# State-space layer's input projections: from 256-column products in threes to a 512-column product and a 256-column one

## The chip, the cores and the metric

One core of one Trainium2 chip runs the whole model in one launch. The metric is the device time of one execution in microseconds (us). Engines are named as in the profile: PE is TensorE's matmul, PEld its weight load, DVE VectorE, ACT ScalarE, POOL GpSimd, SP the queue that issues the DMAs.

## What is computed

The reference runs a first block (attention of two kinds, then a mixture of sixteen experts) on 256 tokens of width 1024, and then two layers of a second block, each a mixer and a feed-forward part. The mixer of the first of these layers is a state-space layer, and it is the part that matters here, cut to its core:

```python
proj = u @ w_in                       # [256,1024] @ [1024,5152]
z   = proj[..., :2048]                # gate
xbc = proj[..., 2048:2048+3072]       # x (2048), B (512), C (512)
xbc = silu(causal_dwconv(xbc, conv_w, conv_b))      # four taps along the tokens
y = ssd_chunked_scan(xs, dt, a, bm, cm) + d_skip * xs
g = y * silu(z), normalised in 4 groups of 512 channels
return g @ w_out
```

All matrix products of this layer are taken in float32 accuracy by splitting each operand into a high part and a low part that TensorE multiplies at full rate: w·h is about wh·hh + wh·hl + wl·hh.

## The kernel before

A weight matrix arrives in **pages** of 1 MiB: `wpage` loads 1024 rows by 256 columns as a tile of 128 partitions by 8 blocks by 256. `split` makes the page's high part `wh` by a cast on ACT (L231) and its low part `wl` by a subtraction on DVE (L232). There are three buffers for each part, so the cast of a page waits until TensorE has done with the third page before it. The activations `hx` lie in one tile of 8 blocks, each with 256 columns of the high part and, right behind them, 256 columns of the low part; `hx[k][0]`, `hx[k][1]` and `hx[k][2]` are the high part, the low part and both together.

`c_proj` takes one page. For each of its two chunks of 128 output channels and each of 8 blocks it issues three products of 256 columns (`three`, L243 to L245): wh with the high part, wh with the low part, wl with the high part. These are 48 matmuls, all into one PSUM bank (two chunks by 256 tokens). In the state-space layer (function `ssd`) nineteen pages go this way: eleven by `xpage` (three of B and C; a fourth is computed elsewhere, as `led[1]`; and eight of x) and eight by `z_group`. `xpage` then runs the convolution straight from the PSUM bank (`conv2`: two ACT operations, L1363, and six DVE operations, L1368), and a Silu on ACT writes the result to its place. `z_group` runs the Silu straight from PSUM into `zs`, of which there is one buffer for all four groups.

`c_proj2` is there already and is used for the up projection of both feed-forward parts. It takes 32 matmuls for a page: wh with both activation parts at once (512 columns, L1335) and wl with the high part (256 columns, L1338). Each chunk has a bank of its own. A copy on ACT (L1342) brings the second half of the bank to SBUF and an addition on DVE (L1343) adds the first half to it.

PSUM has eight banks: two with the tag `cm`, two `cs`, and four accumulators (`ca00` to `ca11`) for the layer's output projection, `down`. In `ssd` the accumulators are allocated by the caller before the layer begins, and the first product goes into them in `out_group(0)`, far into the layer.

The order of the layer in the program: three pages of B and C, x of group 0, decay factors, z of group 0; then for each group g `scan(g)`, the pages of x of group g+1, `scan_end(g)` (gate, sum of squares, norm; its last reading of `zs` is L1616), the pages of z of group g+1. `out_group(0)` follows the z pages of group 2, `out_group(1)` comes within group 3, the other two at the end. A scheduler lays out each engine's queue from this order ahead of the run, and mixes what is independent: the products of the scan stand in TensorE's queue among those of the next pages. Each queue is then worked off strictly in its order. `tc.issue_after(i)` puts what is traced under it behind instruction i of the same engine.

Of the kernel before, what the change touches and what calls it, by code (L numbers as in the profile page):

```python
# [9 lines left out]
F32 = mybir.dt.float32  # L10
# [4 lines left out]
AF = mybir.ActivationFunctionType  # L15
# [152 lines left out]
def tile_model(ctx, tc, A, out):  # L168
# [40 lines left out]
    def wpage(w, c0, n, k0=0, k=8):  # L209

        return page([128, k, n], w[k0 * 128:(k0 + k) * 128, c0:c0 + n].rearrange("(k p) n -> p k n", p=128))
# [23 lines left out]
    last_mm = [None]  # L235
# [801 lines left out]
    def cm(name="cm"):  # L1037
        return psC.tile([128, 512], F32, name=name, tag="cm", bufs=2)
# [283 lines left out]
    def c_proj(pg, ps, hx, parts=1):  # L1322
        wh, wl = split(pg, parts=parts)
        for c in range(pg.shape[2] // 128):
            three(ps[:, 256 * c:256 * c + 256],
                  [(wh[:, k, 128 * c:128 * c + 128], wl[:, k, 128 * c:128 * c + 128]) for k in range(8)], hx, True, True)

    def c_proj2(pg, names, hx, out_):

        wh, wl = split(pg)  # L1330
        for c in range(pg.shape[2] // 128):
            ps = (cm, cs)[c % 2](names)
            cc = slice(128 * c, 128 * c + 128)
            for k in range(8):
                wide = lambda: pe.matmul(ps, lhsT=wh[:, k, cc], rhs=hx[k][2], start=(k == 0), stop=(k == 7))  # L1335
                if k == 0:
                    wide()
                last_mm[0] = pe.matmul(ps[:, :256], lhsT=wl[:, k, cc], rhs=hx[k][0], start=False, stop=False)  # L1338
                if k:
                    last_mm[0] = wide()  # L1340
            o = out_[:, 256 * c:256 * c + 256]
            act.copy(o, ps[:, 256:])  # L1342
            dve.tensor_tensor(o, ps[:, :256], o, ALU.add)  # L1343

    def down(acc_, items, first, last, pl=None):

        ws = [(split(pg, pl, bufs=2) if pl and i else split(pg), pairs, pg.shape[1]) for i, (pg, pairs) in enumerate(items)]
        its = list(enumerate(ws))

        for t, n, (i, ((wh, wl), pairs, n_)) in [(0, n, x) for x in its for n in range(2)] + \  # L1350
                [(1, n, x) for n in range(2) for x in its]:
            ns = slice(512 * n, 512 * n + 512)
            three(acc_[t][n], [sl(pairs[a], lambda u: u[:, nat(t)]) for a in range(n_)],
                  [(wh[:, a, ns], wl[:, a, ns]) for a in range(n_)],
                  first and i == 0, last and i == len(ws) - 1)

    def rpage(w, r0, a=2):
        return page([128, a, D], w[r0:r0 + 128 * a].rearrange("(a p) n -> p a n", p=128))
# [73 lines left out]
            dn(13, 14, 15, pl=fp)  # L1432
            return next_layer(acc_, A["norm_ffn_post_2"][i], *((A["norm_mix_pre_2"][1], lru_lead) if i == 0 else ()))

    def ssd(hx, acc_, led):
        with ExitStack() as es:
            sp3 = es.enter_context(tc.tile_pool(name="ssd_y", bufs=1, reuse_waits="tile"))
            es2 = es.enter_context(ExitStack())
            sp2 = es2.enter_context(tc.tile_pool(name="ssd", bufs=1, reuse_waits="tile"))
# [28 lines left out]
            def xpage(c0, dst):  # L1468

                if c0 == 2048:  # L1470
                    ps = led[1]
                else:
                    ps = (cs if c0 >= 2048 and c0 % 512 else cm)("xbc")
                    c_proj(wpage(w, 2048 + c0, 256), ps, hx)
                y = sp2.tile([128, 2, S], F32, name="cvs", tag="cvs", bufs=2)
                conv2(y, ps, lambda c, a: C("ssd_conv_w_2", 24 * a + c0 // 128 + c),
                      lambda c: C("ssd_conv_b_2", c0 // 128 + c), 4)
                act.activation(out=dst, in_=y, func=AF.Silu)

            xs, zs, ys = {}, {}, {}  # L1480

            def x_group(g):
                xs[g] = sp2.tile([128, 4, S], F32, name="xs", tag="xs", bufs=2)
# [3 lines left out]
            def z_group(g):  # L1487
                zs[g] = sp2.tile([128, 4, S], F32, name="zs", tag="zs", bufs=1)
                for i in range(2):
                    ps = cm("z")  # L1490
                    c_proj(wpage(w, 512 * g + 256 * i, 256), ps, hx)
                    act.activation(out=zs[g][:, 2 * i:2 * i + 2], in_=ps.rearrange("p (c n) -> p c n", c=2), func=AF.Silu)

            for i in range(4):
                xpage(2048 + 256 * i, bc[:, 2 * i:2 * i + 2])
# [122 lines left out]
                ys[g] = split(sq, sp3, "ys", 2, dve if g == 3 else pool, parts=2 if g == 3 else 1)  # L1618

            def out_group(g, pl=None):  # L1620
                down(acc_, [(rpage(A["ssd_w_out_2"][0], 512 * g + 256 * b),
                             [sl(ys[g], lambda u: u[:, 2 * b + a]) for a in range(2)]) for b in range(2)], g == 0, g == 3,
                     pl)
# [3 lines left out]
            for g in range(4):  # L1627
                scan(g)
                if g < 3:
                    x_group(g + 1)  # L1630
                else:
                    out_group(1)
                scan_end(g)
                if g < 3:
                    z_group(g + 1)
                if g == 1:
                    out_group(0)
            out_group(2)
            root_table(sp3, ys[3][0].bitcast(F32)[:, 0, 0:1])
            out_group(3)  # L1640
# [115 lines left out]
            es2.close()  # L1756
            return next_layer(acc_, A["norm_mix_post_2"][1], A["norm_ffn_pre_2"][1], up_lead(1))

    acc0 = accs()
    for t, (xg, v) in enumerate(first):  # L1760
        dve.tensor_scalar(x1[:, t], xg, inv_root(rows2, v[1], D, v[0]), None, ALU.mult)
    xps_.close()
    rw2.close()
    hx, led = ssd(hx, acc0, [ps[0] for _, ps in lead])
    hx, led = ffn(0, hx, led)
    hx, led = lru(hx, led)
    ffn(1, hx, led)
# [18 lines left out]
```

## Time and profile before

| | |
|---|---|
| median of 3 runs | 2274.14 us (2273.88 to 2277.45) |
| the profiled execution's own time | 2269.94 us |
| its span | 2268.1 us |
| busy over the span: PE, PEld, DVE, ACT, POOL | 84%, 61%, 45%, 35%, 11% |
| state-space layer, from its first projection product to its last output product | 1402.1 to 1607.6 us |

The busy shares are averages over stages with different limits: for some 900 us in the middle the expert weights stream in and DVE and ACT are nearly idle. So the rows further down are of the state-space layer's stretch, and of one stretch of the feed-forward part where the other form of the projection runs. Times inside the trace are microseconds from the span's start.

### The profile page before, as it was taken

Reading aid. Unit: us, or ns where it says so; the run is one execution under the profiler, and the core shown is the slowest. Engines: PE = TensorE matmul, PEld = TensorE weight load, DVE = VectorE, ACT = ScalarE, POOL = GpSimd, SP = SyncE. Lnnn points to the kernel's source line nnn. Section 1 sums busy time; section 2 is a strip of 40 time slices with the busy share of each in tenths; the row PEclk is TensorE's granted clock in tenths of the full one; section 3 lists DMA queues with packets and bytes.
Section 4 is the critical chain, followed back from the end, with each engine's and each line's share of the span. In section 5 each row is a group of like instructions: output and inputs, shape, how many; then the busy total and the mean of one; then the engine's idle time right before and its main releaser. Section 6 shows DMA issues by size and latency. Waiting matters only on the chain.

```text
span 2268.1 us, 31933 instructions
## 1 busy us (share of the span) xinstructions
PE 1915.4 (84%) x13582; PEld 1372.4 (61%) x13582; DVE 1017.0 (45%) x1537; ACT 799.7 (35%) x1203; POOL 244.4 (11%) x174
## 2 busy tenths in 40 slices
PE   7999999987666666665666758999999999999998
PEld 4989998842222222121222216987888889888887
DVE  7867664420000000000000005868767767877775
ACT  2445454420000000000000004655666667666564
POOL 0100013100000000000000003010222222032222
PEclk9999999999878888788879788999999999999999
DMA  9357675789999999999999998434565556456552
GB/s 325 113 186 252 215 240 190 273 354 427 426 426 427 425 426 426 426 427 426 426 426 425 426 427 295 151 129 132 175 195 184 188 167 216 142 194 196 185 186 84
DMA packets 202539, 644.30 MB, mean 284 GB/s; under 512 B 8086, under 2 KB 145430, under 8 KB 169754
## 3 DMA queue, kind: packets, MB, share of 16 engines
q1 hardware_dynamic: 202396, 642.25, 74.5%
q8 instruction: 107, 1.75, 0.3%
q14 instruction: 36, 0.29, 0.0%
HBM read 640.91 MB, written 1.05 MB: 283 GB/s over the span
## 4 chain that ended last, share of the span: by engine, by line
PE 54%; DMA 39%; DVE 4%; ACT 2%; issue 1%; POOL 0%; SPq 0%; DVEq 0%; ACTq 0%; POOLq 0%
DMA epage<-in_w_gu 24%; DMA epage<-in_w_dn 14%; PE up L1335 10%; PE up L1338 5%; PE ca L245 4%; PE ca L244 4%; PE ca L243 3%; PE qk L245 2%; PE qk L244 2%; PE qk L243 2%; PE lead L1254 2%; PE xbc L243 1%; PE v L244 1%; PE v L245 1%; PE v L243 1%; PE xbc L244 1%
## 5 line engine op out<-in xcount | busy, mean ns | idle before, releaser
L232 DVE TENSOR_TENSOR wl<-page,wh 128x2048 fp32r<-128x2048 f32 (+2 forms) x191 | 435.3, 2280 | 204.7 <-ACT wh L231 204.2
L1176 PE MATMUL gu<-epage,xeT 128*32 128x512 f32 x2048 | 325.2, 763 | 211.4 <-DMA epage<-in_w_gu 211.1
L231 ACT CAST wh<-page 128x2048 fp32r<-128x2048 f32 (+2 forms) x191 | 357.7, 1874 | 234.3 <-PE ca L245 65.1
L1176 PEld LDWEIGHTS gu<-epage,xeT 128*32 128x32 f32 x2048 | 60.8, 125 | 453.8 <-DMA epage<-in_w_gu 350.3
L1335 PE MATMUL up<-hb,wh 128*128 128x512 f32 x960 | 331.9, 396 | 0.0
L1338 PE MATMUL up<-hb,wl 128*128 128x256 f32 x960 | 248.0, 279 | 0.0
L1187 DVE TENSOR_TENSOR hid<-hid,gu 128x512 f32<-128x512 f32 x16 | 11.0, 688 | 522.6 <-PE gu L1176 522.6
L1186 ACT ACTIVATE hid<-gu 128x512 f32<-128x512 f32 x16 | 9.6, 597 | 630.4 <-PE gu L1176 630.4
L1335 PEld LDWEIGHTS up<-hb,wh 128*128 128x128 f32 x960 | 173.2, 188 | 33.6
L1338 PEld LDWEIGHTS up<-hb,wl 128*128 128x128 f32 x960 | 180.9, 188 | 10.6
L1203 PE MATMUL dn<-epage,hidT 128*32 128x256 f32 x2048 | 149.4, 436 | 43.4 <-DMA epage<-in_w_dn 34.7
L1208 DVE TENSOR_TENSOR ye<-dn,gt 128x256 f32<-128x256 f32 x64 | 27.2, 424 | 255.2 <-PE dn L1203 255.2
L1203 PEld LDWEIGHTS dn<-epage,hidT 128*32 128x32 f32 x2048 | 68.8, 122 | 108.6 <-issue 37.2
L1368 DVE SCALAR_TENSOR_TENSOR cv<-ups,cols,cv 128x255 f32<-128x255 f32 x240 | 117.4, 501 | 27.6 <-ACT cv L1363 26.0
L243 PE MATMUL qk<-hh,wh 128*128 128x256 f32 x384 | 110.1, 287 | 0.0
L244 PE MATMUL qk<-hl,wh 128*128 128x256 f32 x384 | 109.4, 285 | 0.0
L245 PE MATMUL qk<-hh,wl 128*128 128x256 f32 x384 | 108.7, 283 | 0.0
L245 PE MATMUL ca<-wh,hdl 128*128 128x512 f32 x256 | 101.7, 397 | 0.0
L1153 POOL TENSOR_SCALAR part<-sq 128x1 f32<-128x1 f32 x2 | 0.4, 190 | 939.3 <-ACT xeT L276 939.2
L244 PE MATMUL ca<-wl,hdh 128*128 128x512 f32 x256 | 100.9, 394 | 0.0
L243 PE MATMUL ca<-wh,hdh 128*128 128x512 f32 x256 | 100.3, 392 | 0.0
L1210 PE MATMUL ca<-ye,sel 128*128 128x256 f32 x256 | 75.3, 418 | 28.8 <-DVE ye L1208 28.8
(524 smaller groups left out, 3598.8 us busy)
## 6 DMA issues: line engine op xcount, KB each, us to landing
epage<-in_w_gu SPq DMA_DIRECT2D x102, 2048.0 KB, 29.9
epage<-in_w_dn SPq DMA_DIRECT2D x51, 2048.0 KB, 29.9
page<-in_ffn_w_up SPq DMA_DIRECT2D x64, 1024.0 KB, 5.5
epage<-in_w_gu SPq DMA_DIRECT2D x52, 1024.0 KB, 32.6
page<-in_w_in SPq DMA_DIRECT2D x46, 1024.0 KB, 5.8
page<-in_ffn_w_down SPq DMA_DIRECT2D x32, 1024.0 KB, 4.9
epage<-in_w_dn SPq DMA_DIRECT2D x26, 1024.0 KB, 31.8
page<-in_w_ada SPq DMA_DIRECT2D x24, 1024.0 KB, 6.9
```

What stands on the lines that cost most here:

```text
L231: act.copy(hi[p_], v[p_])
L232: (lo or dve).tensor_tensor(lw[p_], v[p_], hi[p_], ALU.subtract)
L243: pe.matmul(ps, lhsT=ah, rhs=bh, start=first and k == 0, stop=False)
L244: pe.matmul(ps, lhsT=ah, rhs=bl, start=False, stop=False)
L245: last_mm[0] = pe.matmul(ps, lhsT=al, rhs=bh, start=False, stop=last and k == n - 1)
L1176: pe.matmul(gu[i][32 * j:32 * j + 32, :], lhsT=xeT[:, k, 32 * e:32 * e + 32], rhs=pg[i][:, 512 * j:512 * j + 512], start=(k == 0), stop=(k ...
L1203: pe.matmul(pd[32 * q:32 * q + 32, bs], lhsT=hT[:, k % 4, k // 4, :], rhs=pg[k // 8][:, 256 * (k % 8):256 * (k % 8) + 256], start=(k < 4), ...
L1210: pe.matmul(acc[t][b // 2][:, bs], lhsT=sel[:, nat(t)], rhs=ye, start=False, stop=(e == NE - 1 and b % 2 == 1))
L1254: pe.matmul(pss[0][:, 256 * c + 128 * t:256 * c + 128 * t + 128], lhsT=pg[:, k, 128 * c:128 * c + 128], rhs=hf[:, k, nat(t)], start=(k == ...
L1335: wide = lambda: pe.matmul(ps, lhsT=wh[:, k, cc], rhs=hx[k][2], start=(k == 0), stop=(k == 7))
L1338: last_mm[0] = pe.matmul(ps[:, :256], lhsT=wl[:, k, cc], rhs=hx[k][0], start=False, stop=False)
L1368: dve.scalar_tensor_tensor(y[:, c, o:], ps[:, 256 * c:256 * c + S - o], wcol(c, j), y[:, c, o:], ALU.mult, ALU.add)
```

## The change

All nineteen pages go through `c_proj2`. Its result is written into the place of the final result: the tile `dst` for x, B and C (the convolution now reads it from SBUF, and the Silu writes over it), and `zs` for z (the Silu works in place). The banks: until the accumulators are needed, pages rotate through the four accumulator banks (`pm` counts them); `accs()` is called only at the first z page of group 2, and from then on both chunks of a page take `cm` banks. `out_group(0)` is put behind the last product of that z page.

```diff
-    def c_proj2(pg, names, hx, out_):
+    def c_proj2(pg, names, hx, out_, banks=None):
...
-            ps = (cm, cs)[c % 2](names)
+            ps = (banks or (cm, cs))[c % 2](names)
...
-    def ssd(hx, acc_, led):
+    def ssd(hx, led):
         with ExitStack() as es:
+            acc_, spare_ = [], [0]
+            def pm(name):
+                if acc_:
+                    return cm(name)
+                spare_[0] += 1
+                i = spare_[0] % 4
+                return psC.tile([128, 512], F32, name=name, tag=f"ca{i // 2}{i % 2}", bufs=1)
...
-                    ps = (cs if c0 >= 2048 and c0 % 512 else cm)("xbc")
-                    c_proj(wpage(w, 2048 + c0, 256), ps, hx)
+                    ps = dst.rearrange("p c n -> p (c n)")
+                    c_proj2(wpage(w, 2048 + c0, 256), "xbc", hx, ps, (pm, pm))
...
-                    ps = cm("z")
-                    c_proj(wpage(w, 512 * g + 256 * i, 256), ps, hx)
-                    act.activation(out=zs[g][:, 2 * i:2 * i + 2], in_=ps.rearrange("p (c n) -> p c n", c=2), func=AF.Silu)
+                    if g == 2 and i == 0:
+                        acc_.extend(accs())
+                    z = zs[g][:, 2 * i:2 * i + 2]
+                    c_proj2(wpage(w, 512 * g + 256 * i, 256), "z", hx, z.rearrange("p c n -> p (c n)"), (pm, pm))
+                    if i == 0:
+                        z_first[0] = last_mm[0]
+                    act.activation(out=z, in_=z, func=AF.Silu)
...
             def out_group(g, pl=None):
+                if not acc_:
+                    acc_.extend(accs())
...
                 if g == 1:
-                    out_group(0)
+                    with tc.issue_after(z_first[0].ins):
+                        out_group(0)
...
-    acc0 = accs()
...
-    hx, led = ssd(hx, acc0, [ps[0] for _, ps in lead])
+    hx, led = ssd(hx, [ps[0] for _, ps in lead])
```

## Rows read from the trace of the kernel before

**Rows 1.** Windows: stretch, length, busy us of PE, PEld, DVE, ACT, POOL, granted clock, DMA.
```profile
1402.14:1607.63 205.49, 198.45 (x1462) 175.95 (x1462) 156.40 (x281) 122.16 (x174) 26.80 (x30) 1.00 0.47 150
1402.14:1446.20 44.06, 44.06 (x366) 43.82 (x367) 37.06 (x56) 27.98 (x36) 14.73 (x24) 1.00 0.78 244
1446.20:1480.69 34.49, 32.94 (x277) 30.12 (x276) 27.64 (x55) 20.83 (x30) 0.00 (x0) 1.00 0.40 124
1480.69:1528.21 47.52, 44.43 (x325) 39.09 (x323) 31.14 (x59) 27.31 (x37) 6.53 (x2) 1.00 0.40 131
1528.21:1563.81 35.60, 33.90 (x280) 30.91 (x279) 29.75 (x56) 21.03 (x30) 0.00 (x0) 1.00 0.46 154
```

**Rows 2.** Waits of PE, 1402.1 to 1607.63: sum in us, times, longest.
```profile
PE ca L243 <- ACT wh L231: 3.2, 2, 1.7
PE st L1554 <- DVE xd L1550: 1.5, 1, 1.5
PE z L243 <- DVE cvs L1368: 1.5, 1, 1.5
PE xbc L243 <- DVE dtu L1460: 0.3, 1, 0.3
```

**Rows 3.** Timeline of PE at these waits: start, duration, form, idle time before.
```profile
1466.60 0.35 PE L243 MATMUL z<-hb,wh 128*128 128x256 f32 x1 [1.46 <-DVE cvs L1368]
...
1484.64 0.28 PE L243 MATMUL xbc<-hb,wh 128*128 128x256 f32 x1
...
1503.62 0.50 PE L243 MATMUL ca<-wh,ysh 128*128 128x512 f32 x1 [1.53 <-ACT wh L231]
...
1548.75 1.19 PE L243 MATMUL ca<-wh,ysh 128*128 128x512 f32 x4 [1.65 <-ACT wh L231]
```

**Rows 4.** Timeline of ACT: casts that a page's last use of a buffer released.
```profile
1419.60 1.90 ACT L231 CAST wh<-page 128x2048 fp32r<-128x2048 f32 x1 [2.42 <-PE xbc L244]
...
1431.12 1.91 ACT L231 CAST wh<-page 128x2048 fp32r<-128x2048 f32 x1 [2.42 <-PE xbc L244]
```

**Rows 5.** Timeline of PE: first product of two up pages, first product behind them.
```profile
1641.61 0.40 PE L1335 MATMUL up<-hb,wh 128*128 128x512 f32 x1
...
1652.80 0.39 PE L243 MATMUL ca<-wh,hdh 128*128 128x512 f32 x1
```

**Rows 6.** Tiles up and ups: duration in ns (min/median/max), first and last start.
```profile
L1342 ACT COPY ups<-up x120: 347/372/374, 1630.2 to 2241.9; 128x256 f32<-128x256 f32 x120
L1343 DVE TENSOR_TENSOR ups<-up,ups x120: 408/417/427, 1630.5 to 2242.4; 128x256 f32<-128x256 f32 x120
...
L1368 DVE SCALAR_TENSOR_TENSOR cv<-ups,cols,cv x240: 465/480/1512, 1633.0 to 2244.0; 128x255 f32<-128x255 f32 x108, 128x254 f32<-128x254 f32 x12
...
L1363 ACT ACTIVATE cv<-ups,cols x120: 587/602/611, 1632.4 to 2242.9; 128x256 f32<-128x256 f32 x120
```

**Rows 7.** Tiles xbc and z: duration in ns (min/median/max), first and last start.
```profile
L1368 DVE SCALAR_TENSOR_TENSOR cvs<-xbc,cols,cvs x66: 465/472/483, 1412.9 to 1550.3; 128x255 f32<-128x255 f32 x22, 128x254 f32<-128x254 f32 x22, 128x253 f32<-128x253 f32 x22
L1363 ACT ACTIVATE cvs<-xbc,cols x22: 544/554/588, 1411.9 to 1546.4; 128x256 f32<-128x256 f32 x22
...
L1492 ACT ACTIVATE zs<-z x8: 578/588/592, 1439.6 to 1567.1; 128x512 f32<-128x512 f32 x8
```

**Rows 8.** Timeline of DVE: low part of a page, and last readings of zs, groups 0 to 2.
```profile
1476.21 2.29 DVE L232 TENSOR_TENSOR wl<-page,wh 128x2048 fp32r<-128x2048 f32 x1 [0.99 <-ACT wh L231]
...
1479.57 1.66 DVE L1616 SCALAR_TENSOR_TENSOR xs<-zs,cols,rb 128x256 f32<-128x256 f32 x4 [0.67 <-PE rb L1614]
...
1515.27 1.65 DVE L1616 SCALAR_TENSOR_TENSOR xs<-zs,cols,rb 128x256 f32<-128x256 f32 x4
...
1562.68 1.66 DVE L1616 SCALAR_TENSOR_TENSOR xs<-zs,cols,rb 128x256 f32<-128x256 f32 x4 [0.67 <-PE rb L1614]
```

**Rows 9.** Timeline of ACT: Silu of both z pages of group 1.
```profile
1483.51 1.07 ACT L1492 ACTIVATE zs<-z 128x512 f32<-128x512 f32 x2
```

More of the change, by code (lines that the diff above doesn't have):

```diff
@@ L1478, in xpage @@
                 act.activation(out=dst, in_=y, func=AF.Silu)
-            xs, zs, ys = {}, {}, {}
+            xs, zs, ys, z_first = {}, {}, {}, [None]
             def x_group(g):
```

## The prediction, made before the change was run

> **What bounds the kernel now.** I read the page's busy shares first, and they mislead here: PE's 84% is a mean over a long stretch that waits for expert weights and others that do not. So the second view is the windows over the state-space layer, where all edits lie. There PE is busy for 198.45 of 205.49 us at the full clock of 2.4 GHz (granted 1.00) in all four stretches shown, with DVE at 76% and ACT at 59% [rows 1]. TensorE sets the pace, and 7.04 us of idle PE is all that can be won beside shorter PE work. Third, the waits: 6.5 of the 7.04 us have four names [rows 2]. Fourth, the timeline puts them in their places [rows 3]: 1.46 us ahead of the z pages of group 1, because the bank they want is still read by the convolution of an x page; 1.53 and 1.65 us where a product of the output projection stands in PE's queue ahead of a z page and waits for the cast of its own page; 1.5 us at the scan's `st`, for `xd` from DVE; and 0.3 us at the very first product. The reader is to see two things. In the first stretch (to 1446.20) PE has no gap at all, so shorter PE work there is won in full. In the group stretches the scan's chain of small DVE and ACT steps runs beside the pages, DVE is at 80% and 84% in the stretches of group 0 and group 2 [rows 1], and whatever is added to DVE there can come back as a wait of PE.
>
> **The pages' products.** Before: casts two pages apart start at 1419.60 and 1431.12, each released by the last use of a buffer, so a page takes 11.52 / 2 = 5.76 us, or 120 ns for each of 48 matmuls [rows 4]. After: the up pages have the same operands and shapes as the new code. Two of them run from 1641.61 to 1652.80, where the next product starts, with DVE and ACT working beside them: 11.19 / 2 = 5.595 us, 350 ns for a pair of 512 and 256 columns [rows 5]. The number of columns is the same (768 for each block and chunk); only the third weight load and its overhead go. Gain 0.165 us a page, 3.1 us for nineteen. Below: nothing, if the pair takes the 360 ns of three single products.
>
> The Trainium skill, TensorE: Matmul & The Clock Gate, section Back-to-back issue gap, puts the gap at N/2.4 plus 2.5 ns. By that rule a page would go from 48 times 109.2 ns to 16 times (215.8 + 109.2) ns, 5.24 to 5.20 us, and nineteen pages would give an estimated 0.8 us. The rows show 120 and 350 ns, so I go by them, but the rule speaks for the small end.
>
> **The evacuation.** Each page gets two ACT copies of 372 ns and two DVE additions of 417 ns [rows 6]: 14.1 us more on ACT and 15.8 us on DVE over the layer. The convolution's operations cost about the same from SBUF as from PSUM: 480 against 472 ns on DVE, 602 against 554 ns on ACT [rows 6, 7], together 0.5 and 1.1 us. The Silu in place is bounded by the same 48 ns, 0.4 us for eight. None of this is on PE. What hides it is DVE's and ACT's idle time, and that is thin. To 1446.20 DVE has 37.06 us of work [rows 1]; 14 additions make it 42.9 in some 42.6 us, although these durations overlap a little in the record. PE doesn't stop for it: three split buffers let it run two pages, 11 us, behind DVE. What comes late first is `xdt` of the first scan, behind which x pages of group 1 can fill in. In the stretch of group 0 eight additions take DVE from 27.64 to 31.0 of 34.49 us.
>
> **The sum, boundary by boundary.** (a) To 1446.20: seven pages, 1.16 us, and the 0.3 us wait of the first product, whose bank is now an accumulator that nobody holds: -1.5.
> (b) To the first x product of group 2 (1484.64). Two things must be over by then. PE's own work: -1.5, four pages -0.66, the 1.46 us wait gone since a bank is now free after a copy and an addition, not after the convolution: -3.6. But z of group 1 cannot be written before the last reading of the single `zs` (L1616, 1479.57 to 1481.23 [rows 8]). Until then its two pages hold all four accumulator banks, as they held both `cm` banks before, and then it was the Silu, 1483.51 to 1484.58, that let PE go on [rows 9, 3]. Now it is copy and addition, 0.8 us after that reading and not 3.4 us (-2.6); the chain to it starts 1.5 us earlier and carries four additions more (+1.7). That makes -2.4, which is later than -3.6 and so decides: another -0.9.
> (c) Group 1, to the next scan: four pages, -0.66, and the 1.53 us wait, since `out_group(0)` now stands behind the first z page, whose parts have long been split. The second z page must wait for L1616 (1515.27 to 1516.92 [rows 8]), because two `cm` banks hold only one page. Its cover is `out_group(0)`: 48 products of 512 columns at 233 ns (two thirds of a pair's 350), 11.2 us, with the z page 16.8 us. PE was free at 1502.1 (1503.62 less 1.53), now at 1499.7, so it has work to 1516.5; the reading ends at 1516.92 less 2.4 plus two additions, 1515.4. Nothing is lost: -2.2.
> (d) Group 2: four pages, -0.66; the 1.65 us wait may go as well, as the z page no longer needs a bank that a convolution holds. Against that stand the banks: x and the first z page have two, so each half page (2.8 us of PE) must see the previous half but one carried off. Copy and addition take 0.8 us; with one low part of 2.29 us ahead of the addition in DVE's queue [rows 8] it is 3.1, a wait of 0.3, and there are six such points: +1.9. The second z page again waits for L1616, with `out_group(1)` as cover. Together -0.4.
> (e) From the last z page to the end of the layer PE has two output groups to fill with and of the idle time there only part of the 0.5 us that has no name above: nothing.
> Sum -1.5 - 0.9 - 2.2 - 0.4 = **-5.0 us**. Later layers are not touched. On the profiled execution's own time, 2269.94 us (its span of 2268.1 and 1.8 around it), that gives 2264.9; this execution lies 4.2 us under the median of the runs, so on the median of 2274.14 it gives **2269.1 us**, 0.22% less. A measurement here tells about 0.2%, 4.5 us, from no change.
> The ends: all idle time gone as well as the pages' gain, -10.2 us; at the other end the dearest of the rivals.
>
> **The rivals.**
> DVE takes it back (22%). In the stretches of groups 0 and 2, where DVE is fullest, all eight additions (3.3 us) lie in the scan's chain and PE runs out of independent pages. For: 84% before, and a single `zs` that ties the pages to the chain. Against: half of these additions come after the chain's last reading, and PE has an output group as filler in group 2. With 3.3 us twice, less the 1.7 already counted, the sum is -0.1: 2274.0.
> The two banks decide (13%), and it is slower. After the accumulators are taken, a half page waits for ACT's copy behind a cast (1.9 us [rows 4]) and for DVE's addition behind a low part (2.29 us): 0.8 + 1.9 + 2.3 - 2.8 = 2.2 us, six times, 13.2 in place of 1.9: +6.3, 2280.4. It ends above the old time from 1.15 us at each point. For: DVE and ACT serve their queues in order, and the scan's steps come first in the program. Against: the up pages run two pages without a gap with the same evacuation, but they have four banks.
> The new form isn't faster here (9%): 360 ns for a pair, because scan products keep cutting into the pages. The sum without its 3.1 us is -1.9: 2272.2. The skill's rule above leans this way; the rows of the up pages lean against it.
>
> **How the numbers follow.** The forecast has 56%, with its own range from -9.5 to -2.5 us (all waits gone, or bank waits twice as long); four fifths of it lie beyond -4.5 us, which gives 45% for faster. The first and third rival are within 0.2% nearly always, as is the rest of the forecast: 41%. The bank rival, and a little of the first, gives 14% for slower. The range 2264.5 to 2278.5 leaves out the best few per cent of the forecast and the dear half of the bank rival.
>
> **What would show it.** Right: two x pages ahead of 1445 take 11.2 us and not 11.5; the scan's first `xT` starts 1.5 us earlier; no wait ahead of the z pages of group 1, and none of PE for a cast before those of group 2; products of `out_group(0)` between the two z pages of group 2. Wrong: idle PE at x or z products, released by the DVE addition or the ACT copy (L1343, L1342), in group 2; longer idle time at `st`; a pair at 360 ns; PE idle in the layer above 7 us.

## The result and the profile after

The changed kernel takes 2292.4 us (2285.04 to 2298.49) against 2274.14 for the kernel before in the same session: a ratio of 1.0079 [1.0059, 1.0099], 0.8% slower, where 0.2% faster was forecast. The profiled execution took 2298.49 us, span 2296.7. From its first projection product to its last output product the state-space layer takes 227.62 us and not 205.49, +22.1 us. What follows it takes as long as before (660.2 and 660.5 us to the end of the span). The profiled execution is the slowest of the five and also has 6.7 us more ahead of the layer (1408.85 against 1402.14), where none of the changed operations lie; over all traces of this document the layer starts between 1400.4 and 1408.9 us. So the times below are counted from the layer's first product.

Windows of after, with the same boundaries as [rows 1]: the whole layer, then from each scan's first `xT` to the next (stretch, length, busy us of PE, PEld, DVE, ACT, POOL, granted clock, DMA):

```profile
1408.85:1636.47 227.62, 207.11 (x1160) 166.09 (x1158) 173.82 (x320) 134.31 (x212) 24.46 (x30) 0.93 0.42 136
1408.85:1446.33 37.48, 37.48 (x227) 33.05 (x226) 36.74 (x66) 30.11 (x47) 15.79 (x24) 1.00 0.74 233
1446.33:1486.19 39.86, 37.86 (x242) 30.81 (x241) 34.36 (x63) 26.81 (x40) 0.00 (x0) 1.00 0.56 181
1486.19:1538.43 52.24, 47.14 (x259) 37.29 (x258) 37.18 (x73) 28.14 (x47) 4.78 (x2) 0.93 0.29 91
1538.43:1576.66 38.23, 35.97 (x211) 28.01 (x210) 30.13 (x57) 22.98 (x35) 0.00 (x0) 0.96 0.50 176
1576.66:1636.47 59.81, 48.66 (x228) 36.94 (x226) 35.41 (x63) 26.26 (x46) 3.89 (x4) 0.83 0.19 59
```

Against [rows 1] the first two stretches together are 1.2 us shorter (77.34 against 78.55; the first `xT` stands at another place among the z pages, so they are taken together), the third is 4.7 us longer, the fourth 2.6, and the last, 43.82 us before (1563.81 to 1607.63), is 16.0 us longer. Two things are to be seen. PE is idle for 20.5 us and not 7.0. And PE is busy for 8.7 us more although the pages should save it 3.1: the granted clock, 1.00 throughout before, is 0.93, 0.96 and 0.83 in the last three stretches. So +13.5 us are idle time, and the other +8.7 are PE work at the lower clock (some 11.8) less the saving. The clock's part can be counted in another way: inside the four stretches at half clock PE is busy for 23.4 us, and half of that is 11.7.

The waits of PE in the layer, which answer to [rows 2]:

```profile
PE ssq L1622 <- ACT xs L1618: 5.7, 3, 2.4
PE st L1568 <- DVE xd L1564: 3.6, 2, 1.9
PE ca L243 <- ACT wh L231: 2.8, 2, 2.3
PE rb L1628 <- DVE dgz L1627: 2.6, 1, 2.6
PE z L1335 <- ACT wh L231: 2.0, 1, 2.0
PE ca L243 <- ACT ysh L231: 1.7, 1, 1.7
```

With four more, 2.1 us together, these are the whole 20.5. `ssq` (sums of squares) and `rb` (the norm) belong to the end of a scan's chain. At this end of the last scan PE waits for 9.3 us in all. The kernel before has two small waits there, which are in its list of waits but not in [rows 2]:

```profile
PE ca L243 <- ACT ysh L231: 0.5, 1, 0.5
PE rb L1614 <- DVE dgz L1613: 0.2, 1, 0.2
```

So this chain was just covered before, with next to nothing in reserve, and now lies open. Two places explain it.

**Behind the first scan.** Timeline of PE:

```profile
1485.41 0.50 PE L1335 MATMUL z<-hb,wh 128*128 128x512 f32 x1 [1.99 <-ACT wh L231]
...
1487.73 0.51 PE L1338 MATMUL z<-hb,wl 128*128 128x256 f32 x2 [0.70 <-DVE wl L232]
...
1493.53 1.10 PE L1568 MATMUL st<-xd,bn 128*128 128x512 f32 x2 [1.70 <-DVE xd L1564]
...
1494.70 0.40 PE L1335 MATMUL xbc<-hb,wh 128*128 128x512 f32 x1
```

Counting z products from the start of the layer, the one at 1485.41 is the first of group 2: both pages of group 1 are through by 1483.43. They hold all four accumulator banks, since `zs` is still to be read, so no x page of group 2 has a bank. The queue fills the place with a z page of group 2, whose cast and low part aren't there; 22 of its 32 products run by 1491.83, the other ten from 1511.33 on. Timelines of DVE (last reading of `zs` of group 0, the next scan's `xd`, the additions of z of group 1) and of ACT (their copies):

```profile
1487.60 1.65 DVE L1630 SCALAR_TENSOR_TENSOR xs<-zs,cols,rb 128x256 f32<-128x256 f32 x4
...
1490.97 2.42 DVE L1564 TENSOR_TENSOR xd<-xdt,dec 128x512 f32<-128x512 f32 x1
1493.31 1.41 DVE L1343 TENSOR_TENSOR zs<-z,zs 128x256 f32<-128x256 f32 x4
```

```profile
1490.29 1.18 ACT L1342 COPY zs<-z 128x256 f32<-128x256 f32 x4
```

The reading ends at 1489.25, and x of group 2 starts 5.5 us behind it. It starts 85.85 us behind the layer's first product; before it was 82.50 [rows 1, 3].

**At the last scan.** Timelines of PE, DVE and ACT:

```profile
1580.57 0.40 PE L243 MATMUL ca<-wh,ysh 128*128 128x512 f32 x1
1582.87 1.93 PE L1568 MATMUL st<-xd,bn 128*128 128x512 f32 x2 [1.90 <-DVE xd L1564]
1583.81 1.42 PE L1335 MATMUL z<-hb,wh 128*128 128x512 f32 x1
...
1590.79 0.40 PE L1335 MATMUL z<-hb,wh 128*128 128x512 f32 x1
1591.03 0.63 PE L1577 MATMUL csb<-csd,of 128*128 128x512 f32 x2
```

```profile
1576.87 1.66 DVE L1630 SCALAR_TENSOR_TENSOR xs<-zs,cols,rb 128x256 f32<-128x256 f32 x4 [1.18 <-PE rb L1628]
...
1582.64 0.74 DVE L1343 TENSOR_TENSOR zs<-z,zs 128x256 f32<-128x256 f32 x2
```

```profile
1579.57 0.64 ACT L1342 COPY zs<-z 128x256 f32<-128x256 f32 x2
```

The second z page of group 3 stands between the scan's `st` and its `csb`. The first page of that group fills both `cm` banks and can't leave them until `zs` of group 2 has been read for the last time (1576.87 to 1578.5); its copies follow at 1579.57, its additions only at 1582.64. `out_group(1)`, 48 products, was to cover this wait, and it is used up there: 46 of them stand between the `st` of group 2 and this one, where before there were 12. The scan's next product, `csb`, comes 8.2 us behind `st`; before it was half a microsecond:

```profile
1566.59 1.09 PE L1554 MATMUL st<-xd,bn 128*128 128x512 f32 x2
1567.12 0.80 PE L1563 MATMUL csb<-csd,of 128*128 128x512 f32 x1
```

At the far end the filler is missing:

```profile
1606.45 0.40 PE L245 MATMUL ca<-wh,ysl 128*128 128x512 f32 x1
1608.40 0.61 PE L1622 MATMUL ssq<-kc,xs 128*128 128x1 f32 x4 [1.55 <-ACT xs L1618]
...
1614.73 2.72 PE L1622 MATMUL ssq<-kc,xs 128*128 128x1 f32 x12 [2.36 <-ACT xs L1618]
1620.09 1.19 PE L1628 MATMUL rb<-dgz,kc 128*128 128x128 f32 x4 [2.63 <-DVE dgz L1627]
1623.03 0.79 PE L243 MATMUL ca<-wh,ysh 128*128 128x512 f32 x1 [1.75 <-ACT ysh L231]
```

At 1606.85 the last product of `out_group(2)` ends. From there to 1623.03, where `out_group(3)` starts, PE has only the chain's own small products; before, output products stood between all of these. Windows of 2 us over PE alone (stretch, length, busy, granted clock, DMA):

```profile
1606.00:1608.00 2.00, 0.84 (x4) 1.00 0.44 152
1608.00:1610.00 2.00, 0.81 (x8) 1.00 0.00 0
...
1612.00:1614.00 2.00, 0.37 (x4) 0.50 0.96 329
...
1626.00:1628.00 2.00, 2.00 (x7) 0.66 0.00 0
1628.00:1630.00 2.00, 2.00 (x10) 1.00 0.00 0
```

Behind this thin stretch the granted clock falls from 1.00 (2.4 GHz) to 0.50 (1.2 GHz), and the 48 products of `out_group(3)` begin at 0.50: they take 13.44 us (1623.03 to 1636.47) and not 11.48 (1596.15 to 1607.63).

### The profile page after: what moved, and what is told of

Its sections match the earlier page's. It is cut to its first block, busy times and chain, and to the rows that moved or that the text cites. A ratio compares the mean times of both kernels' runs of the same rounds, so it can differ in the third digit from the quotient of the medians.

```text
span 2296.7 us, 31374 instructions
## 1 busy us (share of the span) xinstructions
PE 1938.6 (84%) x13278; PEld 1373.0 (60%) x13278; DVE 1034.2 (45%) x1575; ACT 812.0 (35%) x1241; POOL 243.2 (11%) x174
## 4 chain that ended last, share of the span: by engine, by line
PE 54%; DMA 38%; DVE 5%; ACT 2%; issue 1%; SPq 0%; POOL 0%; DVEq 0%; ACTq 0%; POOLq 0%
DMA epage<-in_w_gu 24%; DMA epage<-in_w_dn 13%; PE up L1335 10%; PE up L1338 5%; PE ca L244 4%; PE ca L245 4%; PE ca L243 3%; PE lead L1254 2%; PE xbc L1335 2%; PE qk L245 2%; PE qk L244 2%; PE qk L243 2%; PE z L1335 1%; DVE wl L232 1%; PE gu L1176 1%; PE v L243 1%
## 5 line engine op out<-in xcount | busy, mean ns | idle before, releaser
L1176 PE MATMUL gu<-epage,xeT 128*32 128x512 f32 x2048 | 330.4, 776 | 208.8 <-DMA epage<-in_w_gu 208.7
L1338 PEld LDWEIGHTS up<-hb,wl 128*128 128x128 f32 x960 | 180.9, 188 | 10.6
## 6 DMA issues: line engine op xcount, KB each, us to landing
epage<-in_w_gu SPq DMA_DIRECT2D x102, 2048.0 KB, 29.5
epage<-in_w_dn SPq DMA_DIRECT2D x51, 2048.0 KB, 29.5
```

The source lines that it names most:

```text
L1176: pe.matmul(gu[i][32 * j:32 * j + 32, :], lhsT=xeT[:, k, 32 * e:32 * e + 32], rhs=pg[i][:, 512 * j:512 * j + 512], start=(k == 0), stop=(k ...
```

## The experiments

Two main theories, so named in the expectations. **A**: the wide page is no slower; it costs where its destination (the single `zs`) or its banks (two `cm` banks once the accumulators are taken) are held by somebody, because then it moves within PE's fixed order and uses up the filler. **B**: the copies and additions that come with each page load ACT and DVE and delay the scan's chain wherever the page stands. "Wide" is the new form of a page, "narrow" the old one. A third, **C**, came up with e5 and e11: two `cm` banks are too few for any wide page beside the scan.

All results; each ratio is to the kernel before in the same session, whose median was between 2272.76 and 2274.80 us. The columns on the right are from one trace of each kernel. `st` is the first `st` product of the four scans, in us from the layer's first product; "fill" is from the last `st` to the first product of `out_group(3)`.

| kernel | median us | ratio | st of the scans | fill | layer |
|---|---|---|---|---|---|
| before | 2274.14 | | 46.8, 81.3, 128.7, 164.4 | 29.6 | 205.5 |
| after: 19 pages wide | 2292.40 | 1.0079 [1.0059, 1.0099] | 43.5, 84.7, 132.3, 174.0 | 40.2 | 227.6 |
| e1: B, C and x, 11 pages | 2270.23 | 0.9985 [0.9976, 0.9995] | 45.7, 82.8, 122.0, 162.0 | 28.2 | 203.2 |
| e2: z, 8 pages | 2285.74 | 1.0059 [1.0042, 1.0077] | 46.4, 85.2, 124.8, 164.5 | 40.5 | 219.2 |
| e3: none wide, evacuation added | 2310.04 | 1.0169 [1.0152, 1.0186] | 55.2, 97.2, 153.9, 193.8 | 36.4 | 243.6 |
| e4: 13 pages before the accumulators | 2268.77 | 0.9983 [0.9974, 0.9993] | 43.5, 84.8, 127.0, 162.8 | 29.5 | 203.8 |
| e5: these and x of group 3 | 2279.34 | 1.0020 [1.0010, 1.0029] | 43.5, 84.8, 127.0, 168.7 | 31.0 | 213.3 |
| e6: after, last z page moved | 2286.66 | 1.0052 [1.0035, 1.0068] | 43.5, 85.5, 132.7, 174.6 | 31.4 | 219.8 |
| e7: B, C, x of groups 0 to 2, 9 pages | 2266.59 | 0.9963 [0.9949, 0.9977] | 45.7, 82.8, 122.0, 159.3 | 29.5 | 200.2 |
| e8: before, order of out_group(0) alone | 2273.84 | 0.9998 [0.9988, 1.0007] | 46.8, 81.3, 128.8, 164.5 | 29.5 | 205.5 |
| e9: after, two zs, 4 page buffers | 2288.80 | 1.0070 [1.0048, 1.0092] | 46.2, 89.0, 127.8, 168.8 | 31.9 | 213.8 |
| e10: after, 4 page buffers | 2304.01 (one run) | | 46.2, 85.3, 132.7, 174.4 | 37.7 | 226.4 |
| e11: after, x of group 3 in cm and cs | 2285.74 | 1.0053 [1.0034, 1.0073] | 43.5, 85.5, 132.6, 171.2 | 36.3 | 220.5 |
| e12: after without the additions | 2284.16 | 1.0051 [1.0036, 1.0066] | 45.4, 82.8, 130.8, 169.7 | 34.3 | 217.1 |
| e13: e7 and z of group 0, 11 pages | 2264.64 | 0.9955 [0.9941, 0.9969] | 43.6, 82.2, 121.3, 157.2 | 29.5 | 198.2 |
| e14: e7 and z of group 1, 11 pages | 2269.41 | 0.9979 [0.9970, 0.9988] | 45.7, 82.8, 125.0, 160.7 | 29.6 | 201.7 |

**Which pages (e1, e2).** Each undoes the half of the change that concerns the other kind of page. e1:

```diff
-                    c_proj2(wpage(w, 512 * g + 256 * i, 256), "z", hx, z.rearrange("p c n -> p (c n)"), (pm, pm))
+                    c_proj(wpage(w, 512 * g + 256 * i, 256), ps, hx)        # with ps = cm("z")
```

> Only the eleven pages of x, B and C take the 512-column form; the z pages stay as before (one cm bank a page, Silu from PSUM). Theory A (the z pages: with two cm banks and one zs, the second z page of groups 2 and 3 cannot be computed before the last reading of zs, is pushed into the next scan, and the filler runs out): the loss is gone, 2271 to 2276 us, layer (first to last projection product) 203 to 208 us. Rival B (the additional ACT and DVE operations lengthen the scan's chain, wherever they are): 22 of 38 of the loss stay, about 2285 us, layer 218 us.

e2 does the same to `xpage`:

> Only the eight z pages take the 512-column form, in the changed kernel's banks; x, B and C as before. Theory A: nearly the whole loss, 2288 to 2296 us, layer 222 to 229 us. Rival B: 16 of 38 of the loss, about 2282 us, layer 215 us.

The x pages alone gain 2.3 us in the layer; the z pages alone lose 13.7, of it 10.9 in the fill, as much as the whole change loses there (10.6). So the last scan's part belongs to z. The other part doesn't divide: the last `st` is 2.4 us earlier with x alone, as before with z alone, and 9.6 us late with both. For e2 the layer of 219.2 us lies between the two expectations, 222 to 229 and 215.

**The load alone (e3).** The kernel before with all its narrow products, and behind each page two copies and two additions into the place that the Silu then writes:

```diff
+                    for c in range(2):
+                        e_ = dst[:, c]                      # zs[g][:, 2 * i + c] for z
+                        act.copy(e_, ps[:, 256 * c:256 * c + 256])
+                        dve.tensor_tensor(e_, ps[:, 256 * c:256 * c + 256], e_, ALU.add)
```

> The kernel before, with its 256-column products, its banks and its order, and beside that each page's two ACT copies and two DVE additions, written to the place of the result and overwritten by the Silu (their values are not used). Theory A: at most 3 us slower than before, 2274 to 2277 us, layer 205 to 209 us. Rival B: the whole loss and the page gain not there, 2292 to 2300 us, layer 224 to 232 us.

The layer grows by 38.1 us, far beyond what A allowed and beyond B's 232 us too: the load is not harmless. Nor is it B's simple price for each page, since e1 and e7 carry 22 and 18 of these 38 pairs and are faster than before. In e3 each pair sits between a page and the release of its bank, and most pages have only the two `cm` banks, so this run can't separate load from banks.

**Early and late pages (e4, e5, e7).** Pages narrow again from the point on where the accumulators are taken: in e4 x of group 3 and z of groups 2 and 3, in e5 only these z pages; in e7 all z pages and x of group 3.

```diff
+                elif acc_:
+                    ps = (cs if c0 >= 2048 and c0 % 512 else cm)("xbc")
+                    c_proj(wpage(w, 2048 + c0, 256), ps, hx)
                 else:
                     ps = dst.rearrange("p c n -> p (c n)")
```

> The changed kernel, but the six pages behind the first use of the accumulators (x of group 3, z of groups 2 and 3) go the old way, one bank a page. Thirteen pages stay wide. Theory A: the loss of groups 2 and 3 goes, what group 0 lost stays (some 3 us of PE lag at the scan of group 1): 2272 to 2278 us, layer 203 to 210 us. Rival B: 26 of 38 of the loss stay, about 2287 us, layer 220 us.

> The changed kernel with only the four z pages of groups 2 and 3 in the old way (one cm bank a page, Silu from PSUM); all x pages stay wide, those of group 3 in the two cm banks. Theory A (z pages that cannot run ahead of the last reading of zs): 2268 to 2275 us, layer 202 to 209 us, no z product between st and csb of the last scan. Rival C (the two cm banks are too few for any wide page beside the scan, x of group 3 too): still slower, 2280 to 2287 us, layer 213 to 220 us.

> The wide form only for the nine pages of B, C and x of groups 0 to 2, in the four idle accumulator banks; x of group 3 and all z pages the old way; out_group(0) behind the first z page of group 2. Theory A: wide pages cost nothing where they have four banks and a place of their own for the result; nine page gains of 0.165 us and the 1.5 us waits: 2267 to 2271 us, layer 199 to 203 us. Rival B: 18 of 38 of the loss less the page gain, 2279 to 2283 us.

e7 beats both kernels: nine pages with four idle banks and a destination that nobody holds, 5.3 us off the layer. e4 has four more of the same early kind, those of z, and is 3.6 us slower than e7. The layers of e1, e4 and e7 lie in the ranges that A gave, their times 0.4 to 3.2 us below. e5 adds the two x pages that have only `cm`: another 9.5 us, 5.9 of them before the last `st`; its layer of 213.3 us is where C had it, and A is refuted for these pages.

**The place of the last page (e6).** The second z page of group 3 is traced behind `scan(3)`:

```diff
                 scan(g)
+                if g == 3:
+                    z_group(3, (1,))
...
-                    z_group(g + 1)
+                    z_group(g + 1, (0,) if g == 2 else (0, 1))
```

> The changed kernel with all its wide pages, banks and evacuations; only the second z page of group 3 stands behind the last scan in the program instead of ahead of it, so that the scheduler can lay its products among the scan's and not in front. Theory A: st and csb of the last scan come together again and the z page is its filler; 8 to 16 us of the loss go: 2276 to 2284 us, layer 212 to 219 us. Rival B (evacuation work in the chain): nothing to 3 us, 2289 to 2295 us, layer 224 to 229 us.

No operation fewer, and the fill falls from 40.2 to 31.4 us. The layer is 7.9 us shorter, just under the 8 to 16 that A gave. Timeline of PE in e6: `csb` now follows `st`, with the z page behind it.

```profile
1575.01 1.10 PE L1569 MATMUL st<-xd,bn 128*128 128x512 f32 x2 [1.90 <-DVE xd L1565]
1575.55 0.79 PE L1578 MATMUL csb<-csd,of 128*128 128x512 f32 x1
1576.18 0.39 PE L1335 MATMUL z<-hb,wh 128*128 128x512 f32 x1
```

So it is the place, not the work, that opened the chain. The last `st` stays late (174.6): another cause.

**The single `zs` (e9, e10).** A second buffer for `zs` needs room, so one of the five page buffers goes; e10 is the control that has only that.

```diff
-    NPAGE = 5
+    NPAGE = 4
...
-                zs[g] = sp2.tile([128, 4, S], F32, name="zs", tag="zs", bufs=1)
+                zs[g] = sp2.tile([128, 4, S], F32, name="zs", tag="zs", bufs=2)
```

> The changed kernel with two zs buffers, so that a z page can be carried off while the scan still reads the last group's zs; to make room in SBUF there are four page buffers and not five (the next run has that alone). Theory A (the lock on the single zs puts the z pages late and the last one into the last scan): from st of the last scan to the first product of out_group(3) 28 to 32 us as before, not 40; layer 8 to 15 us shorter than the control's. Rival B (the evacuation work itself): within 3 us of the control.

> Control for the run with two zs buffers: the changed kernel with four page buffers and not five. Both theories: layer 227 to 231 us, as the changed kernel's or a little longer.

Against the control the layer is 12.6 us shorter, the last `st` 5.6 us earlier and the fill 5.8 us shorter. The first x product of group 2 in e9, then in e10:

```profile
1482.40 0.39 PE L1335 MATMUL xbc<-hb,wh 128*128 128x512 f32 x1
```

```profile
1492.23 0.39 PE L1335 MATMUL xbc<-hb,wh 128*128 128x512 f32 x1
```

That is 75.1 and 86.5 us behind the layer's first product, with the same pages and additions: so the held `zs` does keep x of group 2 back. (The `st` of group 1 is 3.7 us later in e9, so not every part gains.) The time of the whole program doesn't show the gain, since four page buffers cost elsewhere: what follows the layer takes 666.6 us in e9 and 670.1 in e10, and 660.2 in after. e10 is a single run, so only the two traces are compared; its layer of 226.4 us is just below the 227 to 231 expected.

**Banks and additions (e11, e12).** e11 gives the two x pages of group 3 a `cm` and a `cs` bank; e12 copies the first half of each bank and adds nothing, so that the high part by the low part is left out of the result.

```diff
-                    c_proj2(wpage(w, 2048 + c0, 256), "xbc", hx, ps, (pm, pm))
+                    c_proj2(wpage(w, 2048 + c0, 256), "xbc", hx, ps, (cm, cs) if acc_ else (pm, pm))
```

```diff
-            act.copy(o, ps[:, 256:])
-            dve.tensor_tensor(o, ps[:, :256], o, ALU.add)
+            if banks:
+                act.copy(o, ps[:, :256])
```

> The changed kernel; x of group 3 takes its two chunks' banks from cm and cs (two buffers each, four banks) and not both from cm. Theory C (two banks are too few for the wide pages of group 3): st of the last scan 3 to 6 us earlier than in the changed kernel (174 us from the first product), total 2286 to 2289 us. Rival B (evacuation work, whatever the banks): st at 173 to 176 us, 2290 to 2295 us.

> The changed kernel without the DVE additions in the state-space layer: one ACT copy carries off the first half of each bank, the second half (high weights by low activations) is computed and left out of the result. All products, banks and the single zs stay. Rival B (DVE's 15.8 us of additions lie in the chain): st of the last scan back to 163 to 167 us, layer 8 us or more shorter, 2278 to 2284 us. Theory A (order and banks): st at 171 to 175 us, the last scan still 38 to 41 us long, 2288 to 2293 us.

Each takes back a part: 7.1 us of the layer's 22.1 by more banks for two pages, 10.5 by leaving out the additions. In e12 x of group 2 starts 78.6 us behind the layer's first product, 7.3 us earlier than in after. For the last `st` both results lie between the theories: 171.2 us where C gave 168 to 171 and B 173 to 176, and 169.7 where B gave 163 to 167 and A 171 to 175. Neither makes the whole page form pay.

**The order alone (e8).** The kernel before with `out_group(0)` put behind the first z page of group 2.

```diff
-                    out_group(0)
+                    with tc.issue_after(z_first[0].ins):
+                        out_group(0)
```

> The kernel before with one thing of the change: out_group(0) stands behind the first z page of group 2. Both theories: the 1.53 us wait ahead of the z pages goes, 2271 to 2274 us, layer 203.5 to 205.5 us. If the order alone carries the gain of the two partial kernels that were faster, it is 2268 to 2270 us, layer 201 to 203 us.

Nothing: 0.9998, all milestones within 0.1 us. The wait ahead of the z pages did go (3.2 us in two waits are 1.7 in one), but a new one of 1.0 us ahead of a z product came in its place.

**Free or held destination (e13, e14).** What separates e4 from e7: z pages as load, or their held destination. e13 adds to e7 only group 0's z pages (nobody reads `zs` yet), e14 only group 1's.

```diff
+                    if g == 0:                               # e14: g == 1
+                        z = zs[g][:, 2 * i:2 * i + 2]
+                        c_proj2(wpage(w, 512 * g + 256 * i, 256), "z", hx, z.rearrange("p c n -> p (c n)"), (pm, pm))
```

> The nine early pages wide as in the kernel that beat both (layer 200.2 us), and the two z pages of group 0 wide as well: at that time nobody reads the single zs and four accumulator banks are idle. Theory A (a wide page costs only where its destination or its banks are held by somebody): layer 199.5 to 200.5 us, the scans' st of groups 1 to 3 within 0.5 us of 82.8, 122.0 and 159.3 us, ratio to the kernel before 0.995 to 0.998. Rival (load: each page's two additions on DVE delay the scan's chain wherever the page stands): 1 to 2 us more, 201.2 to 202.2.

> The nine early pages wide, and in place of group 0's z pages those of group 1, whose destination zs is held by the reading of group 0 until the gate is through. Theory A: this is where the loss of the kernel with early pages of both kinds wide (203.8 us against 200.2) comes from: st of group 1 1.5 to 2.5 us later than 82.8 us, waits for a cast or a low part among z pages of group 1, layer 202.5 to 204 us, ratio 0.997 to 0.999. Rival (load): the same cost as the z pages of group 0, within 0.5 us of that kernel's layer.

The same number of pages and additions, and 3.5 us between the layers. e13 even beats the 199.5 us that A gave it. The two pairs of pages stand at different places, though: no scan runs beside z of group 0, the first one runs beside z of group 1. So that it is the destination and not the place rests on e9 and e10 and on the trace. Timeline of PE in e14, then the first x product of group 2 in e13:

```profile
1483.73 0.39 PE L243 MATMUL z<-hb,wh 128*128 128x256 f32 x1 [0.35 <-ACT wh L231]
...
1486.06 0.39 PE L245 MATMUL z<-hb,wl 128*128 128x256 f32 x1 [1.82 <-DVE wl L232]
...
1490.43 0.40 PE L1335 MATMUL xbc<-hb,wh 128*128 128x512 f32 x1
```

```profile
1478.86 0.40 PE L1335 MATMUL xbc<-hb,wh 128*128 128x512 f32 x1
```

In e14 the wide z pages of group 1 hold the four accumulator banks, a z page of group 2 is put in front of x of group 2 and waits for its parts, just as in after; x of group 2 starts 83.9 us behind the first product, in e13 74.8. The late `st` is that of group 2 (125.0), not of group 1 as expected: group 1's `st` hangs on the chain through DVE, and it is the x pages behind it that start late. Both layers lie below the ranges that A gave, e14's by 0.8 us.

e13 has the shortest layer; by the whole time it isn't told from e7 (ratios 0.9941 to 0.9969 and 0.9949 to 0.9977). Windows over its layer:

```profile
1404.09:1602.27 198.18, 195.59 (x1288) 165.50 (x1286) 164.23 (x304) 129.06 (x196) 26.61 (x30) 1.00 0.47 156
```

2.6 us of PE idle and not 7.0, the full clock throughout, and 2.9 us less PE work than before, of which eleven pages at 0.165 us explain 1.8. Some 1.6 of the 2.1 us by which its layer beats that of e7 are the clock: in e7 it falls once, from 1543.80 to 1547.21, with PE busy for 3.25 us at half speed. That e13 has no such fall wasn't foreseen. One thing is not tested: no run has narrow pages in the four accumulator banks, so how much of the idle time saved is owed to the free banks alone, and not to the wide form, stays open.

## Why the prediction was wrong

The kernels e13, e4, e5 and after form a staircase, each with the pages of the one before it: 205.5 us before; 198.2 with the eleven pages whose banks and destination are free (-7.3); 203.8 with z of group 1 (+5.6, held destination); 213.3 with x of group 3 (+9.5, two banks); 227.6 with z of groups 2 and 3 (+14.3, both). The steps hold what the clock does too: e4 runs 6.83 us at half clock, e13 none, which is some 3.0 of the 5.6. They are not additive: z of group 1 costs 1.5 us on top of e7 and 5.6 on top of e13, x of group 3 3.0 on top of e7 and 9.5 on top of e4.

By the prediction's own boundaries the loss is -1.3 (a), +4.7 (b), +0.2 (c), +6.0 (d) and +12.5 (e), together +22.1 us where -5.0 was forecast.

*The pages' products: right.* In the first stretch of after, from one cast to the third behind it, which answers to [rows 4]:

```profile
1415.02 1.92 ACT L231 CAST wh<-page 128x2048 fp32r<-128x2048 f32 x1
...
1431.80 1.92 ACT L231 CAST wh<-page 128x2048 fp32r<-128x2048 f32 x1
```

Three pages in 16.78 us, 5.59 a page, as the up pages gave it. The rival that the new form isn't faster here is refuted. By the Trainium skill, TensorE: Matmul & The Clock Gate, section Back-to-back issue gap, whose formula is for a single product by itself, a page would take an estimated 5.20; no run here shows that pace.

*Step (a): right.* PE goes on from the last z product of group 0 43.1 us behind the first product, with an `xT` of 0.35 us among them, and not 44.1: -1.3 without that `xT`, for -1.5 forecast. Of the forecast 0.3 was the wait of the first product. It did go, but it lies ahead of that product, so it was never among the 7.04 us of idle time in the layer: 6.2 us of these have the other three names, and 0.7 are the two small waits of the last scan shown above.

*Step (b): wrong, +4.7 for -0.9.* It saw that the z pages of group 1 hold the four banks until `zs` is read, and took copy and addition to free them 0.8 us after that reading. That term failed: the copies start 1.0 us behind the reading, the additions at 1493.31 stand in DVE's queue behind the next scan's `xd`, and x of group 2 starts 5.5 us behind the reading, before 3.4. The reading itself ends 1.3 us later in the layer than before, for 0.2 forecast. A second `zs` brings x of group 2 to 75.1 us (86.5 in its control e10), no additions to 78.6 (e12), narrow x pages in `cm` banks to 75.6 (e2): it takes the held destination, the additions and the shared banks together. PE's order, which the step took to be unchanged, also moved: the queue put a page of group 2 there that wasn't ready (e14 shows it alone), and it stood astride the next scan. The removed 1.46 us wait for the bank did go; where destinations are free, x of group 2 starts 7.7 us earlier than before (e13).

*Step (c): wrong, +0.2 for -2.2.* From the first x product of group 2 to the `st` of group 2 it takes 46.4 us, before 46.2: nothing gained, and in it fall 6.83 us at half clock, with PE busy for 6.4 of them, some 3.2 us. With z of groups 1 to 3 narrow (e7, e13) that `st` comes 6.7 and 7.4 us earlier than before. The gain was there; with z of group 1 wide that `st` stands at 127.0 us (e4, and e5 still), with z of groups 2 and 3 as well at 132.3 (after). It takes wide x pages in the same banks for that: with z alone wide (e2) it stands at 124.8, 3.9 us earlier than before.

*Step (d): wrong, +6.0 for -0.4* (from one `st` to the next: 41.7 us, before 35.7). Two `cm` banks were priced at 1.9 us for six points of 0.3 (that is 1.8), as waits of PE. No x or z product of after waits for a copy or an addition. What the trace shows is 2.5 us more idle time, 1.9 where `st` waits for `xd` and the rest where the 1.65 us wait for a cast did not go but became 2.26, and 3.6 us more PE work ahead of `st`: 34 output products more, the second z page less, and 3.41 us at half clock. So the cost came through the order, which spends the filler early, and not as waits at banks. x of group 3 alone, in these banks, costs 5.9 us there (e5 against e4), with 17 output products more ahead of `st`. More banks for these pages (e11) return 2.8 of the last `st`'s delay, no additions (e12) 4.3, a second `zs` (e9 against e10) 5.6: the additions, the banks and the held `zs` each carry a part, and the parts overlap. How the delay divides between them stays open, since each run also changes the order of the queues. The rival with the two banks had the side right, but not the mechanism: its sum makes this step +10.9 us by waits at banks, and of the +6.0 none is a wait at a bank; the 12.5 us of (e) were in no rival.

*Step (e): wrong, +12.5 for nothing.* This is the step that failed most: "PE has two output groups to fill with". The prediction doesn't name the two. If `out_group(1)` is one of them, the same 48 products were booked as cover twice, since step (d) had it already; if `out_group(3)` is, it can't fill, as it waits for this chain's own result (1.75 us for `ysh` at 1623.03). Behind the last `st` there were 36 products of `out_group(1)` and 48 of `out_group(2)` before, and 2 and 48 in after. The last z page then slid into the scan (e6 undoes it by its place alone), the fill grew by 10.6 us, and `out_group(3)` started at half the clock, 1.9 us more.

*DVE takes it back*: in the pure form refuted (e1, e7, e13 are faster with 18 to 22 of the 38 pairs), but it isn't nothing, as e3 and e12 show. My theory A was wrong to hold the load harmless; what fits the runs is load that falls on a bank or a buffer which somebody waits for. No single run isolates that.

## What to carry to other kernels

A wide product that saves matmul overhead and pays with an evacuation gained here on the pages whose banks are idle and whose destination is free, and lost on most of the others; go through the pages one by one and ask who holds either, then convert those alone (eleven of nineteen here, ratio 0.9955). Independent work that covers a wait is a stock: book each product as cover once, ask whether it depends on the chain that it is to cover, and see what is left for the last chain. And a scheduler's order is not a constant of the change: a page that can't get a bank is not waited for but overtaken, by whatever comes next and may not be ready.

## What the hardware showed unexpectedly

The clock took about half of the loss. In the kernel before and in e13 the granted clock is 1.00 over the whole layer, with waits of up to 1.65 us; in after it fell to 0.50 four times, first around 1519:

```profile
1516.00:1518.00 2.00, 1.28 (x11) 1.00 0.00 0
1518.00:1520.00 2.00, 1.56 (x8) 0.53 0.88 240
1520.00:1522.00 2.00, 2.00 (x6) 0.50 1.08 374
```

The fall comes behind waits (0.51 us at 1513.76 and 1.76 us at 1516.71) and stays while PE is full again. Not every idle stretch has this: from 1484 to 1486 PE was busy for 0.59 of 2 us and the clock stayed at 1.00. Nor does every single wait: e7 and e13 both have one of 1.5 us ahead of an output product, and the clock falls behind it in e7 and not in e13. PE's busy time in the layer shows the price, some 11.8 us. The Trainium skill, TensorE: Matmul & The Clock Gate, section HAM oscillation — how this bites in real kernels, tells of a kernel whose gaps between bursts bring the lower clock each time, so that the wait is paid once as idle time and again in the products behind it. The trace agrees in the price: of the 22.1 us, 13.5 are idle time and the rest is PE work that takes longer; but not every wait here brings the lower clock.

DVE's `xd` was slowed by POOL. Timelines of DVE and POOL at the last scan of after:

```profile
1579.98 2.74 DVE L1564 TENSOR_TENSOR xd<-xdt,dec 128x512 f32<-128x512 f32 x1
```

```profile
1579.79 2.38 POOL L232 TENSOR_TENSOR ysl<-xs,ysh 128x1024 fp32r<-128x1024 f32 x1 [46.62 <-ACT ysh L231]
```

All four `xd` of the kernel before take 0.68 us. In after those at 1490.97 and 1579.98 start while POOL splits `ysl`, take 2.42 and 2.74 us and end 0.6 us behind POOL's operation, and `st` waits 1.70 and 1.90 us for them; the other two take 0.7. The last `xd` runs into POOL's operation in e1, e2, e5, e6, e10, e11 and e12 as well (2.27 to 2.76 us), and in e4, e7, e13 and e14 it takes 0.7. So a shift in the order can cost two microseconds on DVE without an instruction more. No run moves the POOL operation away, so what the whole loss owes to it isn't measured.
